# Hybrid SSD and pooling layer with a Strassen feed-forward part: norm and split work, loads and weight buffers moved around the borders of its matmul stages

## The chip, the cores and the metric

The kernel runs on one core of a Trainium2 chip, in one launch. The metric is the device time of that launch in microseconds. The kernel before has a median of 1436.09 us in three runs (1435.75 to 1439.99).

## The reference, cut to what matters

One decoder layer is computed for 1024 prompt positions and 8 sample positions together (1032 columns), with model width 1024, in float32. The changed stages are the output projection's end, the second norm and the feed-forward part.

```python
x = x + jnp.concatenate([y_ssd, y_pool], axis=-1) @ w_out      # 2048 -> 1024
hn = rmsnorm(x, norm2_w)
u = hn @ w_up                                                  # 1024 -> 2 * 2816
u, ffn_new = causal_dwconv(u, ffn_buf, ffn_conv_w, ffn_conv_b) # width 3
gate, val = jnp.split(u, 2, axis=-1)
x = x + (jax.nn.silu(gate) * val) @ w_down                     # 2816 -> 1024
...
y = xf * lax.rsqrt(jnp.mean(xf * xf, axis=-1, keepdims=True) + EPS) * w.astype(jnp.float32)
```

Ahead of these stand the first norm, the input projection, the SSD scan with its gate and norm, and the pooling groups; behind them a last RMSNorm. The outputs also hold the new states.

## The kernel before, in words

Channels lie on the 128 partitions and positions along the free axis. Every float32 operand of a matmul is split in a high part (ACT copies it to the matmul's type: line 210 for moving tiles, 140 for weights) and a low part (DVE subtracts: lines 211 and 141), and each product is three matmuls: high by high, high by low, low by high. Weights go by DMA on SP into `raw` (4 buffers), and their parts into `wop` (4 buffers). The pool `big` has 30 buffers of a tile's width for moving tiles, intermediate tiles and loads; `more` has 6. PSUM gives 8 banks `g` to the feed-forward part.

`w_out` adds its product to x in three parts over eight output tiles n. The first two (SSD heads) take all columns; beside their tiles `down_sums` forms sums of w_down's blocks. The third, `w_out_end`, has the pool groups and runs for one half of the columns (516, in two quarters q of 258) and then for the other. A tile takes 24 matmuls, and then DVE adds each quarter from PSUM to x (line 910). ACT squares the half (917) and sends x to DRAM (`x2d`, 919), and POOL sums the squares for n below 6 (922); the last two go through matmuls with ones. Ln and Exp on ACT give `rn`, and `scale` (943) multiplies x by the norm's weight and by rn on DVE.

The feed-forward part multiplies 2 x 2 blocks with seven products p1 to p7 in place of eight. `moving` makes the sums and splits of the moving blocks; `up_weights` loads weight blocks on SP and adds the second block with an accumulating DMA on POOL (1043); `blocks` has the matmuls (1063). For the first three of 22 pairs j, p1 and p2 of all come first (`up_first`), and then the others. `up_close` makes the convolution (ACT 1137, DVE 1139), SiLU and the product; `spill` makes the differences, and `put` (1160) stores seven blocks per two j in DRAM as `td[0]` to `td[10]`.

`down` reads them back: for each product (p1, p2, p5, p6, p7, p4, p3 in this order) `down_ops` issues eleven loads on POOL (1209) into tiles g and splits them. p1 runs over three slices of the inner dimension (4, 4 and 3 tiles) and within them over four output tiles m; the others go over m first. `down_weights` brings the weights (1227), `piece` the matmuls (1239), and `sink` adds results to x2, which `load_x2` has read back on POOL (1256). The last product interleaves the last norm.

What sets the order: instructions are written down in program order, a scheduler with a simulated time line orders each engine's list, and `behind(ins)` lets an instruction be issued only after `ins` in that order. Each engine then runs its own list strictly in order, and tile pools and operands give the waits between engines.

Of the kernel before, what the change touches and what calls it, by code (L numbers as in the profile page):

```python
# [18 lines left out]
P = 128  # L19
# [56 lines left out]
class Kernel:  # L76
# [131 lines left out]
    def split(self, src, hi, lo, lo_eng=None):  # L208
        nc = self.nc
        nc.scalar.activation(hi, src, AF.Copy)  # L210
        (lo_eng or nc.vector).tensor_tensor(out=lo, in0=src, in1=hi.bitcast(F32), op=ALU.subtract)  # L211

# [636 lines left out]
    def w_out(self, pf):  # L849
# [15 lines left out]
        def part(ops, k0, done=None):  # L865
            for n in range(KT):
                if todo:
                    self.down_sums(len(todo), *todo.pop(0))
# [12 lines left out]
        part(ops, 0)  # L881
# [5 lines left out]
        part(ops, 6)  # L887
# [6 lines left out]
        for t in range(2):  # L894
            self.w_out_end(ops, t)

    def w_out_end(self, ops, t):
# [3 lines left out]
        ssq = self.ph.tile([P, TH], F32, tag=("mh", "sb")[t], name=self.nm("ssq"), bufs=1)  # L901
        pb = [self.bank(b) for b in (("pT", "pT"), ("pM", "pY"))[t]]
        for n in range(KT):
            ws = self.load_tile(d["wout"][n][:, 12 * P : 16 * P], 4)
            x = self.x2[n]
            for q in range(2):
# [3 lines left out]
                nc.vector.tensor_tensor(  # L910
                    out=x[:, lo : lo + TQ], in0=x[:, lo : lo + TQ], in1=ps[:, :TQ], op=ALU.add
                )
            if n == 0:
                act = nc.scalar.activation(ssq, x[:, cols], AF.Square).ins
            else:
                sq = self.ph.tile([P, TH], F32, tag=("sa", "v", "v")[n % 3], name=self.nm("sq"), bufs=(1, 2, 2)[n % 3])
# [19 lines left out]
        if t == 0:  # L936
            for n in range(KT):
                self.scale(n, t)
# [14 lines left out]
    def moving(self, pairs, eng, extra=()):  # L953
# [3 lines left out]
        nc = self.nc  # L957
        ops = {p: [] for p in CHAIN}
# [243 lines left out]
    def down_ops(self, p):  # L1202

        ops = []
        for i in range(0, DK, 2):
# [4 lines left out]
            for j in range(m):  # L1210
                t = self.op_tile()
                self.split(st[:, j], t[:, 0], t[:, 1])
# [31 lines left out]
    def down(self):  # L1244
# [4 lines left out]
        ops = self.down_ops("p1")  # L1249
        x2 = []  # L1250

        def load_x2():
            for n in range(KT):
                t = (self.more if n < 6 else self.big).tile([P, TOK], F32, tag="big", name=self.nm("x2"))
                with self.behind(self.loaded):
                    nc.gpsimd.dma_start(t, self.x2d[n])
                x2.append(t)

        us = [self.big.tile([P, 2, TH], F32, tag="big", name=self.nm("U")) for _ in range(2)]
# [285 lines left out]
```

## Time and profile before

| | |
|---|---|
| median of three runs | 1436.09 us |
| profiled execution, its own time | 1441.22 us |
| its span | 1439.4 us |
| mean granted clock of TensorE | 0.978 |
| PE busy | 1371.8 us (95%) |
| DVE, ACT, POOL busy | 972.9, 700.9, 504.1 us |

PE is the matmul engine, DVE VectorE, ACT ScalarE, POOL GpSimd, SP SyncE. Times of rows are microseconds from the start of the span. In a timeline row the idle time ahead of the instruction and what ended it stand in brackets; "x8" is a run of eight like instructions, and the duration is that of the run. PE matmuls overlap, so a run's duration over its count is nearly the step from one to the next.

### The profile page before, as it was taken

Reading aid. Unit: us, or ns where it says so; the run is one execution under the profiler, and the core shown is the slowest. Engines: PE = TensorE matmul, PEld = TensorE weight load, DVE = VectorE, ACT = ScalarE, POOL = GpSimd, SP = SyncE. Lnnn points to the kernel's source line nnn. Section 1 sums busy time; section 2 is a strip of 40 time slices with the busy share of each in tenths; the row PEclk is TensorE's granted clock in tenths of the full one; section 3 lists DMA queues with packets and bytes.
Section 4 is the critical chain, followed back from the end, with each engine's and each line's share of the span. In section 5 each row is a group of like instructions: output and inputs, shape, how many; then the busy total and the mean of one; then the engine's idle time right before and its main releaser. Section 6 shows DMA issues by size and latency. Waiting matters only on the chain.

```text
span 1439.4 us, 26582 instructions
## 1 busy us (share of the span) xinstructions
PE 1371.8 (95%) x10312; PEld 1321.3 (92%) x10312; DVE 972.9 (68%) x1474; ACT 700.9 (49%) x1408; POOL 504.1 (35%) x569
## 2 busy tenths in 40 slices
PE   8999999797899999999979999999999998999997
PEld 6899878777799999999979999999999998999997
DVE  6475998588863384653678777777777775567743
ACT  6247773366355452311546545554555544544541
POOL 5242576567521104775232222222222213113122
PEclk9999999999899999999989999999999999999999
DMA  6032334334311137776476887878777769457513
GB/s 243 8 99 59 116 122 135 116 121 132 118 36 36 43 91 266 251 224 198 145 206 139 210 207 187 204 187 207 174 184 191 194 219 351 146 182 235 176 47 118
DMA packets 126683, 227.56 MB, mean 158 GB/s; under 512 B 27852, under 2 KB 45084, under 8 KB 126556
## 3 DMA queue, kind: packets, MB, share of 16 engines
q1 hardware_dynamic: 86316, 139.39, 31.2%
q0 software_dynamic: 24208, 61.30, 17.4%
q10 hardware_dynamic: 16032, 25.16, 5.2%
q8 instruction: 81, 1.33, 0.4%
q14 instruction: 46, 0.38, 0.1%
HBM read 169.11 MB, written 45.15 MB: 149 GB/s over the span
## 4 chain that ended last, share of the span: by engine, by line
PE 81%; DVE 9%; DMA 4%; issue 3%; ACT 2%; POOL 1%; SPq 0%; DVEq 0%; ACTq 0%; POOLq 0%
PE g L1063 30%; PE g L1239 16%; PE g L160 10%; PE g L159 10%; PE g L161 10%; DMA mix<-acd 1%; DVE mix L549 1%; DVE mix L504 1%; PE pY L586 1%; DVE xs L482 1%; DVE xs L604 1%; DVE x L295 1%; DMA s<-wup 1%; DVE wop L141 1%; DVE xd L544 1%
## 5 line engine op out<-in xcount | busy, mean ns | idle before, releaser
L1063 PE MATMUL g<-op,wop 128*128 128x258 f32 x3696 | 446.4, 283 | 6.1 <-ACT op L988 5.0
L1063 PEld LDWEIGHTS g<-op,wop 128*128 128x128 f32 x3696 | 445.4, 190 | 6.9 <-ACT op L988 5.2
L1239 PE MATMUL g<-op,wop 128*128 128x258 f32 x1848 | 229.8, 286 | 9.4 <-ACT op L210 5.6
L140 ACT ACTIVATE wop<-raw 128x512 fp32r<-128x512 f32 (+1 forms) x208 | 125.8, 607 | 229.2 <-PE g L161 129.6
L1239 PEld LDWEIGHTS g<-op,wop 128*128 128x128 f32 x1848 | 226.6, 192 | 11.6 <-ACT op L210 6.0
L159 PE MATMUL g<-hh,wop 128*128 128x344 f32 x696 | 227.2, 326 | 4.4 <-ACT u L467 3.8
L161 PE MATMUL g<-hh,wop 128*128 128x344 f32 x696 | 226.5, 325 | 0.0
L160 PE MATMUL g<-hl,wop 128*128 128x344 f32 x696 | 225.7, 324 | 0.0
L141 DVE TENSOR_TENSOR wop<-raw,wop 128x512 fp32r<-128x512 f32 (+1 forms) x186 | 135.9, 736 | 116.2 <-ACT wop L140 111.1
L140 ACT ACTIVATE wop<-s 128x512 fp32r<-128x512 f32 (+1 forms) x136 | 83.4, 620 | 144.3 <-PE g L1063 50.9
L159 PEld LDWEIGHTS g<-hh,wop 128*128 128x128 f32 x696 | 132.8, 191 | 7.4 <-ACT u L467 4.3
L161 PEld LDWEIGHTS g<-hh,wop 128*128 128x128 f32 x696 | 132.7, 191 | 1.3 <-issue 1.1
L160 PEld LDWEIGHTS g<-hl,wop 128*128 128x128 f32 x696 | 133.0, 191 | 0.6 <-issue 0.5
L1043 POOL DMA_DIRECT2D s<-s x44 | 38.3, 870 | 252.3 <-DVE wop L141 106.9
L1139 DVE SCALAR_TENSOR_TENSOR acc<-u,cst,acc 128x1048 f32<-128x1048 f32 x88 | 115.2, 1309 | 12.6 <-ACT acc L1137 11.1
L141 DVE TENSOR_TENSOR wop<-s,wop 128x512 fp32r<-128x512 f32 (+1 forms) x136 | 91.0, 676 | 35.0 <-ACT wop L140 33.2
L1123 DVE TENSOR_TENSOR u<-u,g 128x258 f32<-128x258 f32 (+2 forms) x176 | 58.3, 354 | 74.1 <-PE g L1063 69.9
L1120 ACT ACTIVATE u<-g 128x258 f32<-128x258 f32 (+2 forms) x220 | 69.5, 340 | 71.9 <-PE g L1063 71.7
L160 PE MATMUL g<-yl,wop 128*128 128x344 f32 x288 | 92.6, 323 | 2.3 <-DVE yl L211 2.3
L161 PE MATMUL g<-yh,wop 128*128 128x344 f32 x288 | 92.5, 322 | 0.0
L159 PE MATMUL g<-yh,wop 128*128 128x344 f32 x288 | 91.8, 322 | 0.0
L1209 POOL DMA_DIRECT2D g<-td x77 | 41.9, 548 | 140.6 <-DVE op L211 67.7
(269 smaller groups left out, 2284.6 us busy)
## 6 DMA issues: line engine op xcount, KB each, us to landing
s<-wup SPq DMA_DIRECT2D x88, 256.0 KB, 3.5
g<-td POOLq DMA_DIRECT2D x77, 258.0 KB, 4.6
raw<-wup SPq DMA_DIRECT2D x66, 256.0 KB, 4.1
raw<-win SPq DMA_DIRECT2D x58, 256.0 KB, 2.6
mix<-acd SPq DMA_DIRECT2D x16, 768.0 KB, 5.7
td<-acc ACTq DMA_DIRECT2D x22, 516.0 KB, 6.0
s<-wup POOLq DMA_DIRECT2D x44, 256.0 KB, 5.5
s<-s POOLq DMA_DIRECT2D x44, 256.0 KB, 3.9
```

What stands on the lines that cost most here:

```text
L140: self.nc.scalar.activation(hi, raw[:, :w], AF.Copy)
L141: lo_eng.tensor_tensor(out=lo, in0=raw[:, :w], in1=hi.bitcast(F32), op=ALU.subtract)
L159: nc.tensor.matmul(ps[:, :n], wh, xh[:, sl], start=(first and k == 0), stop=False)
L160: nc.tensor.matmul(ps[:, :n], wh, xl[:, sl], start=False, stop=False)
L161: nc.tensor.matmul(ps[:, :n], wl, xh[:, sl], start=False, stop=(final and k == last))
L1043: nc.gpsimd.dma_start(t, raw[acc] if acc in raw else w[acc][j], accum_op=ALU.add)
L1063: nc.tensor.matmul(out, a, b, start=(p in OPENS and j == 1), stop=(j == 12), skip_group_check=True)
L1120: a = nc.scalar.activation(out, ps[:, s], AF.Copy, scale=-1.0 if p in ("p5", "p4") else 1.0)
L1123: nc.vector.tensor_tensor(out=out, in0=out, in1=ps[:, s], op=op)
L1139: nc.vector.scalar_tensor_tensor(out=acc, in0=u[:, k : k + FW], scalar=self.c("fw", 3 * n + k), in1=acc, op0=ALU.mult, op1=ALU.add)
L1209: self.loaded = self.nc.gpsimd.dma_start(st[:, j], self.td[i + j][ROW[p]]).ins
L1239: self.pe = nc.tensor.matmul(out, a, b, start=(s == 0 and i == 0 and j == 0), stop=(s == len(PIECES) - 1 and i == nk - 1 and j == 2),).ins
```

## The change

- The w_down sums run beside tiles 0 to 5 of w_out's first part and 1 to 6 of its second (before: all eight of the first and four of the second).
- The first half's scales and splits for p1 and p2 run in pairs beside tiles 1 to 7 of the second half, each group issued after the tile's last add; before, the eight scales ran after the first half.
- The squares and their sums use other buffers of the pooling phase.
- The first four moving tiles of p1 of the down projection are loaded and split in `up_close` of the last pair j, before its first convolution step. The rest of p1 follows in `down`, but td[10] only after the first eight loads of p2.
- x2 is read back in half tiles, four halves before p2's last three loads and twelve after; tiles 5 and 7 (before: 6 and 7) are in `big`.
- The first four weight tiles of the last product use the `wop` pool.

```diff
-        def part(ops, k0, done=None):
+        def part(ops, k0, first, done=None):
             for n in range(KT):
-                if todo:
+                if first <= n < first + 6:
                     self.down_sums(len(todo), *todo.pop(0))
...
-        part(ops, 6)
+        part(ops, 6, 1)
...
-        for t in range(2):
-            self.w_out_end(ops, t)
+        self.w_out_end(ops, 0)
+
+        half = KT // 2
+        self.ops = {p: [] for p in CHAIN}
+
+        def beside(n):
+            if n == 0:
+                return
+            for k in {1: (0, 1), 2: (2, 3), 5: (4, 5), 6: (6, 7)}.get(n, ()):
+                self.scale(k, 0)
+            for k in {3: (0, 1), 4: (2, 3), 6: (4, 5), 7: (6, 7)}.get(n, ()):
+                t = self.op_tile()
+                self.split(self.x2[k][:, :TH], t[:, 0], t[:, 1])
+                self.ops["p1" if k < half else "p2"].append((t[:, 0], t[:, 1]))
+
+        self.w_out_end(ops, 1, beside)
...
-        ssq = self.ph.tile([P, TH], F32, tag=("mh", "sb")[t], name=self.nm("ssq"), bufs=1)
+        ssq = self.ph.tile([P, TH], F32, tag=("sb", "ml")[t], name=self.nm("ssq"), bufs=1)
...
-                sq = self.ph.tile([P, TH], F32, tag=("sa", "v", "v")[n % 3], name=self.nm("sq"), bufs=(1, 2, 2)[n % 3])
+                sq = self.ph.tile([P, TH], F32, tag=("mh", "pf", "pf")[n % 3], name=self.nm("sq"), bufs=(1, 2, 2)[n % 3])
...
+            if beside is not None:
+                with self.behind(add):
+                    beside(n)
...
-        if t == 0:
-            for n in range(KT):
-                self.scale(n, t)
...
-        parts("p1", [x[:, a] for x, _ in pairs])
-        parts("p2", [y[:, a] for _, y in pairs])
-        yield ops
...
+        high = None
+        if j == FT - 1:
+            self.begun = self.down_ops("p1", 0, 4)
+            high = self.high
...
-            nc.scalar.activation(acc, u[:, 0:FW], AF.Identity, bias=self.c("fb", n), scale=self.c("fw", 3 * n))
+            with self.behind(high):
+                nc.scalar.activation(acc, u[:, 0:FW], AF.Identity, bias=self.c("fb", n), scale=self.c("fw", 3 * n))
...
-        ops = self.down_ops("p1")
...
+        ops += self.down_ops("p1", len(ops), DK - 1)
+        second = self.down_ops("p2", 0, 8)
+        ops += self.down_ops("p1", DK - 1)
...
-            if p != "p1":
+            if p == "p2":
+                ops = second + self.down_ops(p, len(second))
+                load_x2([(n, t) for n in range(KT) for t in range(2) if (n % 2, t) != (0, 0)])
+            elif p != "p1":
                 ops = self.down_ops(p)
             if p == "p1":
-                load_x2()
+
+                load_x2([(n, 0) for n in range(0, KT, 2)])
...
-                        both[m, s] = self.down_weights(p, m, s, self.big)
+                        both[m, s] = self.down_weights(p, m, s, self.big if m * NS + s >= 4 else None)
```

DVE's list at the start of w_out's second half, before. x_5187 to x_5201 are the eight tiles of x, g the PSUM banks, op the split moving tiles and wop the weights of w_out; the seven rows ahead of these are seven scales like row 604.

```order
604 L943 SCALAR_TENSOR_TENSOR x_5201<-x_5201,cst,rn_6891 128x516
605 L910 TENSOR_TENSOR x_5189<-x_5189,g_6948 128x258
606 L910 TENSOR_TENSOR x_5189<-x_5189,g_6962 128x258
607 L211 TENSOR_TENSOR op_7224<-x_5187,op_7224 128x516
608 L141 TENSOR_TENSOR wop_7093<-raw_7091,wop_7093 128x512
609 L211 TENSOR_TENSOR op_7227<-x_5189,op_7227 128x516
610 L910 TENSOR_TENSOR x_5191<-x_5191,g_6985 128x258
611 L211 TENSOR_TENSOR op_7230<-x_5191,op_7230 128x516
612 L211 TENSOR_TENSOR op_7233<-x_5193,op_7233 128x516
613 L910 TENSOR_TENSOR x_5191<-x_5191,g_6999 128x258
```

The same place after:

```order
597 L925 TENSOR_TENSOR x_5189<-x_5189,g_6940 128x258
598 L925 TENSOR_TENSOR x_5189<-x_5189,g_6954 128x258
599 L958 SCALAR_TENSOR_TENSOR x_5187<-x_5187,cst,rn_6891 128x516
600 L958 SCALAR_TENSOR_TENSOR x_5189<-x_5189,cst,rn_6891 128x516
601 L141 TENSOR_TENSOR wop_7101<-raw_7099,wop_7101 128x512
602 L925 TENSOR_TENSOR x_5191<-x_5191,g_6979 128x258
603 L925 TENSOR_TENSOR x_5191<-x_5191,g_6993 128x258
604 L958 SCALAR_TENSOR_TENSOR x_5191<-x_5191,cst,rn_6891 128x516
605 L958 SCALAR_TENSOR_TENSOR x_5193<-x_5193,cst,rn_6891 128x516
606 L141 TENSOR_TENSOR wop_7140<-raw_7138,wop_7140 128x512
607 L925 TENSOR_TENSOR x_5193<-x_5193,g_7018 128x258
608 L925 TENSOR_TENSOR x_5193<-x_5193,g_7032 128x258
```

The clump of eight scales is gone. Pairs of scales stand behind the adds of tiles 1 and 2 instead, and DVE adds those tiles first.

ACT's list at the border of the up and the down projection, before. acc are the tiles of `up_close` for the last pair, u_12758 and u_12761 its sums out of PSUM, g_13021 the first tile read back and op_13024 its split.

```order
1086 L1120 ACTIVATE u_12761<-g_12785 128x258
1087 L1160 DMA td_13010<-acc_12743 128x516
1088 L188 ACTIVATE acc_12997<-acc_12997 128x1048
1089 L181 ACT_TABLE_LOAD
1090 L1120 ACTIVATE u_12761<-g_12786 128x258
1091 L140 ACTIVATE wop_13188<-raw_13186 128x512
1092 L1137 ACTIVATE acc_13002<-u_12761,cst 128x1048
1093 L210 ACTIVATE op_13024<-g_13021 128x516
1094 L210 ACTIVATE op_13027<-g_13021 128x516
```

The part of the list after in which the first splits for p1 stand (op_12999 to op_13011):

```order
1069 L140 ACTIVATE wop_12907<-s_12777 128x512
1070 L210 ACTIVATE op_12999<-g_12996 128x516
1071 L210 ACTIVATE op_13002<-g_12996 128x516
1072 L140 ACTIVATE wop_12937<-s_12774 128x512
1073 L1131 ACTIVATE u_12761<-g_12847 128x258
1074 L210 ACTIVATE op_13008<-g_13005 128x516
1075 L210 ACTIVATE op_13011<-g_13005 128x516
1076 L1131 ACTIVATE u_12761<-g_12848 128x250
1077 L1131 ACTIVATE u_12761<-g_12848 128x8
1078 L140 ACTIVATE wop_12967<-raw_12780 128x512
1079 L1131 ACTIVATE u_12758<-g_12785 128x258
1080 L1131 ACTIVATE u_12758<-g_12786 128x250
```

The copies L210 stood behind the table load and the last L1137; four of them stand now among the evacuations (L1131, before L1120) of the last up pair.

POOL's list behind p1's loads, before. g are the tiles read back, td_13010 is td[10] and x the tiles of x2.

```order
474 L1209 DMA g_13057<-td_12493 128x516
475 L1209 DMA g_13066<-td_13010 128x516
476 L1256 DMA x_13075<-x2d 128x1032
477 L1256 DMA x_13077<-x2d 128x1032
...
483 L1256 DMA x_13089<-x2d 128x1032
484 L1209 DMA g_13431<-td_7914 128x516
485 L1209 DMA g_13431<-td_8357 128x516
```

And after, where td_13028 is td[10]:

```order
482 L1226 DMA g_13093<-td_11459 128x516
483 L1226 DMA g_13102<-td_13028 128x516
484 L1278 DMA x_13111<-x2d 128x516
485 L1278 DMA x_13113<-x2d 128x516
486 L1278 DMA x_13115<-x2d 128x516
487 L1278 DMA x_13117<-x2d 128x516
488 L1226 DMA g_13459<-td_11976 128x516
489 L1226 DMA g_13459<-td_12493 128x516
```

Before, the load of td[10] and eight loads of x2 stood ahead of p2's first load. Now eight loads of p2 (the last two are shown first) stand ahead of td[10], and x2's halves come behind it.

## Rows read from the trace of the kernel before

**Rows 1.** The page: busy time of each engine, its share of the span, and instructions.

```profile
PE 1371.8 (95%) x10312; PEld 1321.3 (92%) x10312; DVE 972.9 (68%) x1474; ACT 700.9 (49%) x1408; POOL 504.1 (35%) x569
```

**Rows 2.** Waits of PE over the whole span, by what ended them: total us, times, longest.

```profile
PE g L1239 <- ACT op L210: 5.6, 2, 4.1
PE g L1063 <- ACT op L988: 5.0, 1, 5.0
PE g L159 <- DVE x L910: 4.6, 2, 3.3
...
PE g L1239 <- DVE op L211: 1.4, 2, 0.7
```

**Rows 3.** Windows: busy time and number of instructions of each engine, then the granted clock, the DMA engines' busy share and GB/s.

```profile
710.00:720.00 10.00, 7.63 (x62) 7.22 (x60) 10.00 (x16) 6.95 (x19) 4.01 (x2) 1.00 0.28 86
720.00:730.00 10.00, 7.79 (x52) 7.82 (x53) 7.18 (x14) 2.67 (x5) 4.22 (x3) 0.83 0.58 183
750.00:760.00 10.00, 7.63 (x43) 7.63 (x44) 8.97 (x17) 3.47 (x6) 2.04 (x3) 0.66 0.76 150
1150.00:1180.00 30.00, 30.00 (x252) 30.00 (x252) 22.19 (x35) 15.33 (x35) 6.32 (x14) 1.00 0.64 219
1190.00:1200.00 10.00, 7.25 (x39) 6.95 (x40) 9.13 (x13) 3.70 (x6) 6.20 (x13) 0.66 0.91 327
1200.00:1210.00 10.00, 10.00 (x86) 10.00 (x85) 6.29 (x11) 5.76 (x10) 3.16 (x7) 1.00 1.03 405
1390.00:1400.00 10.00, 7.83 (x50) 7.42 (x49) 5.50 (x10) 6.53 (x15) 2.54 (x2) 0.83 0.13 47
```

**Rows 4.** Timeline of PE in the second half of w_out's end: its first matmul, and the two before which PE stood longest.

```profile
705.49 0.47 PE L159 MATMUL g<-ph,wop 128*128 128x258 f32 x1
...
712.87 0.39 PE L159 MATMUL g<-ph,wop 128*128 128x258 f32 x1 [1.26 <-DVE x L910]
...
722.21 0.35 PE L159 MATMUL g<-ph,wop 128*128 128x258 f32 x1 [3.32 <-DVE x L910]
```

**Rows 5.** Timeline of PE at the start of the up projection, and of ACT's copy of accumulated weights there.

```profile
752.37 11.26 PE L1063 MATMUL g<-op,wop 128*128 128x258 f32 x72 [5.03 <-ACT op L988]
...
764.71 1.56 PE L1063 MATMUL g<-op,wop 128*128 128x258 f32 x9 [1.09 <-ACT u L1120]
...
751.16 0.63 ACT L140 ACTIVATE wop<-s 128x512 fp32r<-128x512 f32 x1 [4.88 <-DMA s<-s]
```

**Rows 6.** Timeline of PE from the last up matmuls into the down projection's p1 and p2.

```profile
1186.74 1.23 PE L1063 MATMUL g<-op,wop 128*128 128x258 f32 x9
1192.07 2.09 PE L1239 MATMUL g<-op,wop 128*128 128x258 f32 x8 [4.09 <-ACT op L210]
1194.84 32.37 PE L1239 MATMUL g<-op,wop 128*128 128x258 f32 x256 [0.69 <-DVE op L211]
1228.73 0.74 PE L1239 MATMUL g<-op,wop 128*128 128x258 f32 x4 [1.51 <-ACT op L210]
1230.21 11.55 PE L1239 MATMUL g<-op,wop 128*128 128x258 f32 x92 [0.74 <-DVE op L211]
```

**Rows 7.** Timeline of PE at the start of the last product, and of ACT there.

```profile
1394.82 0.51 PE L1239 MATMUL g<-op,wop 128*128 128x258 f32 x2 [1.95 <-ACT wop L140]
1395.54 5.50 PE L1239 MATMUL g<-op,wop 128*128 128x258 f32 x31 [0.22 <-DVE wop L141]
...
1394.15 3.53 ACT L140 ACTIVATE wop<-s 128x512 fp32r<-128x512 f32 x7
```

**Rows 8.** Timeline of ACT at the end of the up projection, and of POOL's loads of td for p1.

```profile
1188.15 1.28 ACT L181 ACT_TABLE_LOAD   x1
...
1190.25 1.25 ACT L1137 ACTIVATE acc<-u,cst 128x1048 f32<-128x1048 f32 x1
1191.40 1.14 ACT L210 ACTIVATE op<-g 128x516 fp32r<-128x516 f32 x2
...
1169.94 2.21 POOL L1209 DMA_DIRECT2D g<-td  x4 [8.98 <-PE g L1063]
...
1189.49 0.55 POOL L1209 DMA_DIRECT2D g<-td  x1 [11.66 <-DMA td<-acc]
```

**Rows 9.** DMA issues of the page: count, KB each, median us from issue to landing.

```profile
g<-td POOLq DMA_DIRECT2D x77, 258.0 KB, 4.6
```

**Rows 10.** Timeline of DVE in the second half of w_out's end.

```profile
707.06 5.42 DVE L943 SCALAR_TENSOR_TENSOR x<-x,cst,rn 128x516 f32<-128x516 f32 x8 [1.57 <-ACT rn L188]
...
716.76 1.46 DVE L211 TENSOR_TENSOR op<-x,op 128x516 fp32r<-128x516 f32 x1
718.14 1.77 DVE L141 TENSOR_TENSOR wop<-raw,wop 128x512 fp32r<-128x512 f32 x1
...
721.66 0.74 DVE L910 TENSOR_TENSOR x<-x,g 128x258 f32<-128x258 f32 x2
722.32 0.68 DVE L141 TENSOR_TENSOR wop<-raw,wop 128x512 fp32r<-128x512 f32 x1
...
732.62 0.42 DVE L910 TENSOR_TENSOR x<-x,g 128x258 f32<-128x258 f32 x1 [1.01 <-PE g L161]
```

**Rows 11.** Timeline of POOL there: the first two of the five sums of squares, and the last.

```profile
715.28 4.09 POOL L922 TENSOR_TENSOR ssq<-ssq,sq 128x516 f32<-128x516 f32 x2 [18.05 <-ACT sq L917]
...
727.88 1.30 POOL L922 TENSOR_TENSOR ssq<-ssq,sq 128x516 f32<-128x516 f32 x1 [1.68 <-ACT sq L917]
```

More of the change, by code (lines that the diff above doesn't have):

```diff
@@ L209, in split @@
         nc = self.nc
-        nc.scalar.activation(hi, src, AF.Copy)
+        act = nc.scalar.activation(hi, src, AF.Copy).ins
         (lo_eng or nc.vector).tensor_tensor(out=lo, in0=src, in1=hi.bitcast(F32), op=ALU.subtract)
+        return act
     def rsqrt(self, out, sums, scale):
@@ L879, in part @@
                     done(n)
-        part(ops, 0)
+        part(ops, 0, 0)
         ops = []
@@ L893, in w_out, with w_out_end @@
         self.x2d = self.dram.tile([KT, P, TOK], F32, name="x2d")
-        for t in range(2):
-            self.w_out_end(ops, t)
-    def w_out_end(self, ops, t):
+        self.w_out_end(ops, 0)
[11 more added lines that the diff above has]
+        self.w_out_end(ops, 1, beside)
+    def w_out_end(self, ops, t, beside=None):
         nc, d = self.nc, self.d
         cols = slice(t * TH, (t + 1) * TH)
-        ssq = self.ph.tile([P, TH], F32, tag=("mh", "sb")[t], name=self.nm("ssq"), bufs=1)
+        ssq = self.ph.tile([P, TH], F32, tag=("sb", "ml")[t], name=self.nm("ssq"), bufs=1)
         pb = [self.bank(b) for b in (("pT", "pT"), ("pM", "pY"))[t]]
@@ L909, in w_out_end @@
                 self.mm3(ps, ws, ops, lo, TQ)
-                nc.vector.tensor_tensor(
+                add = nc.vector.tensor_tensor(
                     out=x[:, lo : lo + TQ], in0=x[:, lo : lo + TQ], in1=ps[:, :TQ], op=ALU.add
-                )
+                ).ins
             if n == 0:
@@ L953, in moving @@
     def moving(self, pairs, eng, extra=()):
-        nc = self.nc
-        ops = {p: [] for p in CHAIN}
+        nc, ops = self.nc, self.ops
         a, b = slice(0, TH), slice(TH, TOK)
@@ L1200, in down_sums, with down_ops @@
         mix("p3", blk["12"], blk["12"], s2, ALU.subtract)
-    def down_ops(self, p):
+    def down_ops(self, p, first=0, end=DK):
         ops = []
-        for i in range(0, DK, 2):
+        for i in range(first, end, 2):
             m = min(2, DK - i)
@@ L1211, in down_ops @@
                 t = self.op_tile()
-                self.split(st[:, j], t[:, 0], t[:, 1])
+                self.high = self.split(st[:, j], t[:, 0], t[:, 1])
                 ops.append((t[:, 0], t[:, 1]))
@@ L1242, in piece, with down, load_x2 @@
                 ).ins
-    def down(self):
+    def down(self, ops):
         nc, d = self.nc, self.d
         NM, NS = KT // 2, len(PIECES)
-        ops = self.down_ops("p1")
[L1250 to L1254, printed above, removed]
+        ops += self.down_ops("p1", len(ops), DK - 1)
+        second = self.down_ops("p2", 0, 8)
+        ops += self.down_ops("p1", DK - 1)
+        x2 = [None] * KT
+        def load_x2(halves):
+            for n, t in halves:
+                if x2[n] is None:
+                    x2[n] = (self.big if n in (5, 7) else self.more).tile([P, TOK], F32, tag="big", name=self.nm("x2"))
                 with self.behind(self.loaded):
-                    nc.gpsimd.dma_start(t, self.x2d[n])
-                x2.append(t)
+                    self.loaded = nc.gpsimd.dma_start(x2[n][:, half(t)], self.x2d[n][:, half(t)]).ins
+        half = lambda t: slice(t * TH, (t + 1) * TH)
         us = [self.big.tile([P, 2, TH], F32, tag="big", name=self.nm("U")) for _ in range(2)]
-        half = lambda t: slice(t * TH, (t + 1) * TH)
         def sink(p, m, q, ps):
@@ L1417, in phase_ffn @@
                 moving = self.moving([(x2[i], x2[i + half]) for i in range(half)], nc.vector, extra)
+                first = self.up_first(self.ops)
+                next(first)
                 ops = next(moving)
-                first = self.up_first(ops)
-                next(first)
-                next(moving)
                 self.x2 = None
@@ L1428, in phase_ffn @@
                 self.table_set(EXPLN)
-                self.down()
+                self.down(self.begun)
 _INS = {
```

## The prediction

> **What bounds the kernel now.** I read the page first. Its busy line [rows 1] has PE at 1371.8 of 1439.4 us, so PE is idle for 67.6 us, and no other engine is busy for more than 972.9. The kernel is a line of matmuls with holes, and a change is worth what it does to PE's holes and to PE's clock after them. Next, the waits of PE by what ended them [rows 2]. Those in reach of this change are the wait for DVE's adds in w_out (L910, 4.6 us), for the moving tiles of the up projection (ACT L988, 5.0) and for the moving tiles of the down projection (ACT L210, 5.6, DVE L211, 1.4): 16.6 us, and a wait for weight tiles at the last product, told below. In w_out's first two parts, where the w_down sums are moved, the engines' orders are the same in both kernels, so I cost that part at nothing.
>
> Then the windows [rows 3]. A full stretch (1150 to 1180) takes 252 matmuls in 30 us, 0.119 us each; 1200 to 1210 takes 86 in 10, 0.116 each. Behind four of PE's stops, in 720 to 730, 750 to 760, 1190 to 1200 and 1390 to 1400, the granted clock is 0.83, 0.66, 0.66 and 0.83, a mixture of 1.2 and 2.4 GHz. So each of these stops costs more than its idle time. The stops before them lasted 3.32 [rows 4], 5.03 [rows 5], 4.09 [rows 6] and 1.95 us [rows 7]; a stop of 1.26 us [rows 4] was followed by full clock.
>
> **The down border, the largest term.** Before, the last up matmul ends at 1187.97 and the first L1239 starts at 1192.07: 4.09 idle. Eight matmuls then take 2.09 us where 8 x 0.117 = 0.94 would do; 0.69 idle; 256 take 32.37 where 29.95 would do [rows 6]. The loss in p1 is 4.09 + 1.15 + 0.69 + 2.42 = 8.35 us. What PE waits for is ACT's copy of the first moving tile. ACT reaches it at 1191.40 because a table load of 1.28, an evacuation, a weight copy and the 1.25 us activation L1137 stand ahead of it in its order; its data were asked for at 1169.94 [rows 8], where the median load lands in 4.6 us [rows 9]. So it's ACT's order and nothing else. The change moves the first four loads with their copies and subtractions ahead of that group, and interleaves p1's first 24 matmuls with the last up matmuls. PE then has p1's first tiles before it needs them.
>
> Cost of the moved part: four copies at 0.57 [rows 8] and four subtractions at 0.68 (as the lo part in [rows 10]), 2.3 us of ACT and 2.7 of DVE, sooner. In 1150 to 1180 ACT is busy for 15.3 of 30 us and DVE for 22.2 [rows 3], so both have room. But they stand ahead of the last L1137, so the last `up_close`, its spill and td[10] can come up to 2.3 us later. That matters only for the eleventh moving tile, and the change puts this one last and gives p2's eight loads its place in POOL's queue. Before, POOL stood 11.66 us on that td load [rows 8] with x2's loads and all of p2's behind it. After, POOL goes on at once with p2's eight loads, and only then waits.
>
> Next, p2's start: 1.51 + 0.74 = 2.25 us idle, for ACT's and DVE's halves of the split [rows 6]. The loads of these tiles were queued behind x2's eight transfers on POOL. They go ahead of them now, so most of this goes. Against it I set up to 2 us for new short waits, at the third slice of p1 (which needs td[10]) or where U is evacuated in a clump. Sum here: 8.35 + 2.25 = 10.6 at most, and I take 9.5; the lower bound is 4.1, if td[10] comes late enough for a new stop like the old one in p1's third slice, with the half clock behind it: 10.6 - 4.09 - 2.42.
>
> **The last product.** Before, PE stands for 1.95 and 0.22 us at 1394.82, and 31 matmuls take 5.50 us where 3.6 would do [rows 7]: 4.1 us. ACT makes the weight copies in a run of seven from 1394.15, 3.53 us [rows 7]; by its order they wait for large tiles that the product before gives back. Four of twelve weight tiles now come from the pool of weight buffers, which are free once p4 has passed them, so the first tile's weights and one of the next are ready. The fifth still comes behind the release: about 1.1 us of wait (two copies at 0.5) stays. I take 2.5; bounds 1 (the same wait, one tile on) and 4.1.
>
> **The norm border.** Before, DVE runs eight scales in one clump of 5.42 us, and then eight splits and the weights' lo parts between the adds [rows 10]. PE stands 1.26 us at 712.87 and 3.32 us at 722.21 [rows 4], both for an add that came late, and goes on at half clock for some 3 us (about 1.5 lost). All that could be gained by spreading is 1.26 + 3.32 + 1.5 = 6.1 us. But DVE's work isn't less. For the eight tiles of the second half it is 16 adds at 0.37, and eight lo parts, eight scales and eight splits at 0.68 [rows 10]: 5.9 + 16.3 = 22.2 us, against PE's 8 x 2.86 = 22.8 (24 matmuls at 0.119). Where tiles 1, 2 and 5 carry a pair of scales DVE needs 0.74 + 0.68 + 1.36 = 2.8, and for tile 6 with both pairs 4.1. And a DVE instruction beside a POOL sum of squares takes 1.46 or 1.77 us instead of 0.68 [rows 10], so 0.78 to 1.09 more, with five such sums in the half [rows 11]: up to 5 x 0.93 = 4.7, 26.9 in all. In before the loop runs from 705.5 [rows 4] to the end of the last add, 732.62 + 0.42 [rows 10]: 27.5 us. Going through the new order tile by tile I get 23.6 us to the last add where DVE never blocks PE, 25.7 with half of the prolongations and 28.0 with all. Since DVE's instructions now lie closer to POOL's sums (two scales or two splits at every tile from 1 on), I take a value between the last two, 27. That is 0.5 gained; bounds -0.6 and +3.8. The other squares' buffers free the loads of the first up weights from a wait on PE and ACT, but the 5.03 us at 752.37 hang on accumulated weights whose transfer ends at 751.16 [rows 5], a chain that starts when raw buffers come free behind the loop's last lo part. It stays, and moves with the loop. The 1.09 us at 764.71 [rows 5] go half, as p3's weight copy no longer stands ahead of the evacuation. Sum: 1 us; bounds -1.5 and +5.
>
> The Trainium skill, "SBUF — State Buffer", section "SBUF: two separate sides", says that VectorE with two SBUF inputs and a GpSimd instruction that reads SBUF lock each other out of a shared port pair for the whole of an instruction. The two prolonged rows and the POOL pair of 4.09 us (1.30 for one alone) agree with a lock. By this rule each of the five sums could hold DVE for its whole 1.30, 6.5 in all, 28.7 us of DVE work, and the border would gain nothing, where the rows give up to 4.7.
>
> **The sum.** 1 + 9.5 + 2.5 = 13.0 us off the profiled execution: span 1439.4, run 1441.2, so 1428.2 for a run like it. The median of the runs is 1436.09, 5.1 below the profiled run, and the stages that change have no part in that as far as one profile tells; so 1436.1 - 13 = 1423.
>
> **Rivals.**
> - *The norm border opens too.* If POOL's sums seldom meet DVE's two-input instructions, the loop comes near PE's 23.6 us: 3.8 more, and with the whole of the 1.09 and of the last product's 4.1 the gain is 17 to 21: 1415 to 1419. For it: before has DVE busy for only 7.18 us of 720 to 730 [rows 3]. Against it: the load that falls on tile 6, and five sums.
> - *Part of the down border comes back.* ACT's order at the last pair is longer by four copies; if td[10] or the clump of U's evacuations stops PE for 2 to 4 us, the border gives 4 to 6 instead of 9.5, and with nothing at the norm the gain is 4.3 to 8.5: 1428 to 1432. For it: DMA's share is 1.03 in 1200 to 1210, in the stretch in which td[10] is stored and read back [rows 3]. Against it: two thirds of p1, over 20 us of matmuls, stand ahead of the tile's first use.
> - *Nothing in the end.* The stop is only moved: the last up pair's evacuation stands on ACT behind copies that wait for their loads, PE stops there for some 4 us with half clock (8 in all), and 2 to 3 us are left, within 0.3%: 1432 to 1440.
> - *Slower.* One mechanism: in ACT's order the four moved copies stand ahead of evacuations of the last up pair; a load of td that lands after the copy's turn stops ACT, then PE, which has no free PSUM bank. With the median landing of 4.6 us [rows 9] that can't be, as these parts of td were stored over 10 us before; from a landing about 12 us later than that it costs more than the 13 us gained: 1441 and up.
>
> **How the numbers follow.** The forecast (a gain of 8.5 to 17; own range 1419 to 1428) has 0.56, the norm border open 0.12, part given back 0.18, nothing 0.09, slower 0.05. What a measurement can tell from no change is 0.3%, 4.3 us. Faster: 0.56 + 0.12 + 0.18 = 0.86; same 0.09; slower 0.05. The range takes in the forecast, the two rivals beside it and, for the bounds of the terms, a microsecond more at both ends: 1414 to 1433.
>
> **What would show it.** Right: no L1256 matmul waits over 1 us for ACT L210 at the border, the clock there is 1.00, and the window after the last up matmul holds some 85 matmuls per 10 us; POOL's long wait for td stands after p2's loads. In the w_out end, PE's waits for the add are many and short, or one, and together near 5 us; the 5 us for accumulated weights stay. In the last product one wait near 1.1 us, at full clock. Wrong: a stop with half clock anywhere in p1, or a last add at the norm border under 25 us or over 28 us after the half's first matmul.

## The result, and the profile after

The changed kernel takes 1421.78 us (median of four runs, 1417.24 to 1425.72); the kernel before, with a fourth run beside the three told of above, 1438.04 (1435.75 to 1440.89). The ratio is 0.9878, with a 95% interval of 0.985 to 0.9907: 16.3 us less. The forecast was 1423, 13.0 us less. On another chip, five more runs of the changed kernel gave 1423.24 against 1438.52, a ratio of 0.9891 (0.9871 to 0.991), or 15.3 us less. The profiled execution has a span of 1421.1 us, and 1422.84 as its own time.

The waits of PE after, by what ended them (total us, times, longest); they answer to [rows 2]:

```profile
PE pM L940 <- ACT sq L932: 4.3, 2, 2.7
...
PE g L1074 <- ACT op L999: 1.7, 1, 1.7
PE g L1256 <- ACT op L210: 1.7, 1, 1.7
PE g L160 <- DVE yl L211: 1.6, 1, 1.6
PE g L1074 <- DVE op L1004: 1.6, 2, 0.8
PE g L1074 <- DVE u L1134: 1.4, 1, 1.4
...
PE g L1256 <- ACT wop L140: 0.5, 1, 0.5
PE g L159 <- DVE x L925: 0.5, 1, 0.5
```

The wait of the down projection's matmuls (L1256, before L1239) for ACT's split fell from 5.6 to 1.7 us, that for its weights to 0.5. The wait for w_out's adds fell from 4.6 to 0.5, but 4.3 us for the squares of tiles 6 and 7 stand in its place. The wait for ACT's accumulated-weights chain at the start of the up projection (op L999, before L988) fell from 5.0 to 1.7, but waits there for DVE (op L1004 and u L1134, 3.0 us in all) are new; before, one of 1.09 us for ACT stood in their place [rows 5]. PE's stops at the norm border, from the last two tiles' squares on:

```profile
724.97 0.70 PE L940 MATMUL pM<-sq,ones 128*128 128x258 f32 x2 [1.59 <-ACT sq L932]
...
728.78 1.23 PE L940 MATMUL pM<-sq,ones 128*128 128x258 f32 x2 [2.67 <-ACT sq L932]
...
746.38 3.39 PE L1074 MATMUL g<-op,wop 128*128 128x258 f32 x26 [1.72 <-ACT op L999]
750.51 0.98 PE L1074 MATMUL g<-op,wop 128*128 128x258 f32 x6 [0.74 <-DVE op L1004]
...
752.33 5.04 PE L1074 MATMUL g<-op,wop 128*128 128x258 f32 x40 [0.84 <-DVE op L1004]
...
758.78 3.40 PE L1074 MATMUL g<-op,wop 128*128 128x258 f32 x26 [1.42 <-DVE u L1134]
```

The timeline of PE at the down border, which answers to [rows 6]:

```profile
1178.72 1.60 PE L1256 MATMUL g<-op,wop 128*128 128x258 f32 x12
1180.15 1.60 PE L1074 MATMUL g<-op,wop 128*128 128x258 f32 x12
1181.59 0.76 PE L1256 MATMUL g<-op,wop 128*128 128x258 f32 x5
1182.19 1.60 PE L1074 MATMUL g<-op,wop 128*128 128x258 f32 x12
1183.62 36.57 PE L1256 MATMUL g<-op,wop 128*128 128x258 f32 x303
1221.86 13.35 PE L1256 MATMUL g<-op,wop 128*128 128x258 f32 x109 [1.68 <-ACT op L210]
```

No row of p1 has a bracket: its 264 matmuls run without a stop, 17 of them between the last up matmuls and the others behind, at 0.12 us a step. One stop of 1.68 us is left in p2.

The last product, as [rows 7]:

```profile
1379.46 0.51 PE L1256 MATMUL g<-op,wop 128*128 128x258 f32 x2 [0.53 <-ACT wop L140]
1380.18 2.54 PE L1256 MATMUL g<-op,wop 128*128 128x258 f32 x19 [0.22 <-DVE wop L141]
```

The stop of 1.95 us is one of 0.53, and it stands one weight tile later: 21 matmuls of the second output tile follow it, 33 before. Windows, with columns as in [rows 3]:

```profile
720.00:730.00 10.00, 5.46 (x31) 4.65 (x32) 9.82 (x17) 6.25 (x17) 1.64 (x1) 0.84 0.49 152
730.00:740.00 10.00, 10.00 (x66) 9.44 (x65) 5.93 (x10) 6.96 (x17) 2.71 (x3) 0.81 0.97 269
...
1190.00:1200.00 10.00, 10.00 (x85) 10.00 (x85) 8.22 (x15) 4.04 (x8) 4.86 (x9) 1.00 0.93 294
...
1380.00:1390.00 10.00, 9.82 (x75) 9.59 (x76) 7.42 (x14) 6.61 (x16) 1.73 (x4) 1.00 0.16 51
```

The down border and the last product are at full clock; of the changed stages, the norm border alone still has half clock in it (0.84 and 0.81).

Three marks cut the span into stages. The first is the matmul at 705.49 before and 702.16 after. [rows 4] and the prediction call it the first of w_out's second half, but it begins the half's second tile (tile 1): 168 matmuls, seven tiles, lie between it and the first up matmul, and tile 0's run ahead of it. These seven tiles are called the loop below. The second mark is the start of the 169th up matmul. The third is the end of the 33rd matmul of the last product, from where its second output tile could begin; in the changed kernel it lies 12 matmuls, 1.44 us, ahead of the stop shown above. "Again" is a second profile of the same program. The last column is what the prediction took off.

| stage, us | before | after | again | measured gain | forecast |
|---|---|---|---|---|---|
| start to the first mark | 705.49 | 702.16 | 704.29 | 3.3, 1.2 | 0 |
| to the 169th up matmul (norm border) | 59.22 | 56.62 | 56.60 | 2.6 | 1 |
| to the last product's second tile (down border in it) | 628.16 | 618.71 | 617.21 | 9.5, 11.0 | 9.5 |
| to PE's last matmul (last product) | 37.55 | 34.58 | 34.57 | 3.0 | 2.5 |
| rest | 9.0 | 9.0 | 9.0 | 0 | 0 |

Of the 2.6 us at the norm border, 0.1 lie ahead of the first up matmul and 2.5 behind it. There PE stands for 4.7 us in place of 6.1, which is 1.4; the other 1.1 is a faster pace of its matmuls: the granted clock in 750 to 760 is 1.00, where before had 0.66 [rows 3].

### The profile page after: what moved, and what is told of

It is laid out like the page before. It is cut to its first block, busy times and chain, and to the rows that moved or that the text cites. A ratio compares the mean times of both kernels' runs of the same rounds, so it can differ in the third digit from the quotient of the medians.

```text
span 1421.1 us, 26585 instructions
## 1 busy us (share of the span) xinstructions
PE 1364.8 (96%) x10312; PEld 1313.3 (92%) x10312; DVE 968.7 (68%) x1474; ACT 701.1 (49%) x1408; POOL 504.5 (36%) x577
## 4 chain that ended last, share of the span: by engine, by line
PE 79%; DVE 10%; DMA 4%; issue 3%; POOL 2%; ACT 1%; SPq 0%; DVEq 0%; ACTq 0%; POOLq 0%
PE g L1074 30%; PE g L1256 15%; PE g L160 10%; PE g L161 10%; PE g L159 10%; DMA mix<-acd 1%; DVE wop L141 1%; DVE xs L483 1%; DVE mix L550 1%; PE pY L587 1%; DMA st<-st_ssm 1%; DVE x L296 1%; DVE xs L605 1%; DVE mix L505 1%; POOL st L639 1%
## 5 line engine op out<-in xcount | busy, mean ns | idle before, releaser
L1256 PE MATMUL g<-op,wop 128*128 128x258 f32 x1848 | 225.2, 283 | 2.4 <-ACT op L210 1.7
L1256 PEld LDWEIGHTS g<-op,wop 128*128 128x128 f32 x1848 | 222.7, 189 | 3.5 <-ACT op L210 1.9
L141 DVE TENSOR_TENSOR wop<-raw,wop 128x512 fp32r<-128x512 f32 (+1 forms) x186 | 141.3, 765 | 110.5 <-ACT wop L140 108.3
L1156 DVE SCALAR_TENSOR_TENSOR acc<-u,cst,acc 128x1048 f32<-128x1048 f32 x88 | 115.2, 1309 | 12.2 <-ACT acc L1154 10.6
L1134 DVE TENSOR_TENSOR u<-u,g 128x258 f32<-128x258 f32 (+2 forms) x176 | 58.0, 354 | 72.9 <-PE g L1074 66.1
L1131 ACT ACTIVATE u<-g 128x258 f32<-128x258 f32 (+2 forms) x220 | 69.6, 340 | 70.7 <-PE g L1074 70.6
```

Source lines behind the costliest of these rows:

```text
L141: lo_eng.tensor_tensor(out=lo, in0=raw[:, :w], in1=hi.bitcast(F32), op=ALU.subtract)
L1131: a = nc.scalar.activation(out, ps[:, s], AF.Copy, scale=-1.0 if p in ("p5", "p4") else 1.0)
L1134: nc.vector.tensor_tensor(out=out, in0=out, in1=ps[:, s], op=op)
L1156: nc.vector.scalar_tensor_tensor(out=acc, in0=u[:, k : k + FW], scalar=self.c("fw", 3 * n + k), in1=acc, op0=ALU.mult, op1=ALU.add)
L1256: self.pe = nc.tensor.matmul(out, a, b, start=(s == 0 and i == 0 and j == 0), stop=(s == len(PIECES) - 1 and i == nk - 1 and j == 2),).ins
```

## The experiments

Six of these kernels ran once each, for their profile: the sums back (1425.06 us), p2's early loads undone (1428.09), the last product's weight tiles (1424.79), spreading (1430.13), the buffers (1422.62) and p4's loads alone (1423.64). For these the stages are compared, not the run times.

**Is the first stage's difference the w_down sums' doing?** All engines' orders up to there are the same, but the profile after is 3.3 us ahead. One run puts the sums back, and one repeats the changed kernel.

```diff
-                if first <= n < first + 6:
+                if todo:
```

> The changed kernel with the w_down sums beside w_out's tiles where they were before (eight and four). The engines' orders are those of the changed kernel. Theory (the 3.3 us by which the changed kernel's profile is ahead at the first matmul of w_out's second half are chance): all stages behind that point last as in the changed kernel within 0.5 us; ahead of it PE's wait for yl L211 may be anywhere between 1.6 and 2.4 us and the point between 702 and 706. Rival (the moved sums shorten that wait): the wait is 2.3 us and the clock behind it 0.83 again, the point at 705.5.

> The changed kernel itself once more. Its profile, as a second one of the same program, shows how far single stages differ by chance: the first matmul of w_out's second half between 700 and 708 us, PE's wait for op L999 between 1.5 and 4 us, all stages of the down projection within 2 us of the first profile. Run time 1419 to 1426.

With the sums put back, the first mark comes at 704.97, and the wait for yl L211 is 3.04 us, where 1.6 to 2.4 were expected; all stages behind are within 0.5 us of the changed kernel's but two: the 169th up matmul comes at 57.78 for 56.62, and the down stage takes 616.74 for 618.71. The 0.5 us were too narrow. The repeat has 704.29, a wait of 1.95 and a clock of 0.83 behind it. Over the twelve profiles of the changed kernel and its variants, which have the same orders up to there, the mark lies between 700.83 and 707.81, and the wait is at most 3.04; before's 705.49 and 2.32 are inside. So differences of this size come by chance; the moved sums show no effect, as forecast. The expectation of the repeat missed at one place: the wait for op L999 was 1.24, not 1.5 to 4.

**The early copies.** All of p1's tiles back in `down`, the rest unchanged:

```diff
-            self.begun = self.down_ops("p1", 0, 4)
-            high = self.high
+            self.begun = []
```

> The changed kernel without the four early moving tiles of p1: all eleven are loaded and split in the down projection's own part, p2's eight loads still ahead of td[10]. Theory (the stop at the down border was ACT's order, and the early copies removed it): PE waits again for ACT op L210 at the first L1256 for 3.5 to 4.5 us, the clock behind it falls to 0.6 to 0.7 in a 10 us window, and the run is 6 to 9 us slower than the changed kernel. Rival (the stop went because POOL and DMA were freed of x2's loads): the wait stays under 1 us.

Median 1430.43 us (1428.01 to 1433.28), ratio to before 0.9935 (0.9911 to 0.9959): 8.7 us slower than the changed kernel's 1421.78, and 7.2 slower than its second median. Against the kernel before in the same rounds (1440.56) the gain is 10.1 us, where the changed kernel had 16.3 and 15.3, so 5 to 6 us are lost. PE and ACT at the border, and the window behind it:

```profile
1187.88 1.78 PE L1255 MATMUL g<-op,wop 128*128 128x258 f32 x8 [4.09 <-ACT op L210]
1190.66 69.54 PE L1255 MATMUL g<-op,wop 128*128 128x258 f32 x561 [0.99 <-DVE op L211]
```

```profile
1186.06 1.25 ACT L1153 ACTIVATE acc<-u,cst 128x1048 f32<-128x1048 f32 x1
1187.21 1.14 ACT L210 ACTIVATE op<-g 128x516 fp32r<-128x516 f32 x2
```

```profile
1190.00:1200.00 10.00, 9.34 (x61) 9.35 (x62) 8.06 (x13) 3.30 (x6) 3.78 (x7) 0.74 0.64 187
```

The stop of 4.09 is back to the hundredth, ended by the same copy behind the same L1153, with half clock after it: 0.74 in the window, where 0.6 to 0.7 was expected. The down stage takes 624.7 us, 6.8 more than the mean of the two changed profiles (618.0); in the ten profiles that have this border as changed it takes 616.7 to 618.7. The theory holds.

**p2's loads ahead of td[10] and x2.** Here td[10] and all halves of x2 come first on POOL:

```diff
-        ops += self.down_ops("p1", len(ops), DK - 1)
-        second = self.down_ops("p2", 0, 8)
-        ops += self.down_ops("p1", DK - 1)
+        ops += self.down_ops("p1", len(ops))
...
-                load_x2([(n, 0) for n in range(0, KT, 2)])
+                load_x2([(n, t) for n in range(KT) for t in range(2)])
```

> The changed kernel with td[10] and all of x2 loaded ahead of p2's tiles on POOL, as before; x2 still in halves. Theory (p2's early loads are worth the 2.25 us of waits that p2's start had): PE waits for ACT or DVE at p2's start for 2 to 5 us in all, where the changed kernel has 1.7. Rival (they are worth little, since the changed kernel has 1.7 us there still): the wait stays at 1 to 2 us and the span from the last up matmul to p2's hundredth is within 1 us.

PE at p2's start:

```profile
1218.57 0.74 PE L1256 MATMUL g<-op,wop 128*128 128x258 f32 x4 [1.51 <-ACT op L210]
1220.05 11.29 PE L1256 MATMUL g<-op,wop 128*128 128x258 f32 x92 [0.74 <-DVE op L211]
```

These are before's two waits, 1.51 and 0.74, unchanged. The down stage takes 620.1 us, 2.1 more than the mean of the two changed profiles and 1.4 more than the longest of those ten. The order of POOL's queue is what removed them. What stays at this place in the changed kernel is 1.68 us in one profile, 0.20 in the next and none with the sums put back. In the profile that has 1.68 the cause is another: ACT stands for a weight transfer there, and the split of p2's tile is queued behind that copy.

```profile
1220.66 0.63 ACT L140 ACTIVATE wop<-raw 128x512 fp32r<-128x512 f32 x1 [4.13 <-DMA raw<-wdn]
```

**The last product's weight tiles.** All of them back in the large pool:

```diff
-                        both[m, s] = self.down_weights(p, m, s, self.big if m * NS + s >= 4 else None)
+                        both[m, s] = self.down_weights(p, m, s, self.big)
```

> The changed kernel with all of the last product's weight tiles in the large pool, as before. Theory (the four tiles in the weight pool took away most of the stop and with it the half clock): PE waits 1.9 to 2.2 us for the second output tile's weights, the granted clock behind it is below 0.9 in a 10 us window, and from the wait's end to the last matmul the stretch is as in the kernel before; the last product is 2.5 to 3.5 us longer than the changed kernel's. Rival (the early loads of the down projection's start moved that stop too): the wait stays at 0.5 to 0.8 us.

PE and two windows:

```profile
1378.73 5.88 PE L1256 MATMUL g<-op,wop 128*128 128x258 f32 x33 [1.94 <-ACT wop L140]
```

```profile
1370.00:1380.00 10.00, 8.06 (x61) 7.63 (x61) 2.57 (x6) 3.82 (x8) 2.57 (x2) 0.93 0.00 1
1380.00:1390.00 10.00, 10.00 (x73) 9.80 (x71) 6.48 (x13) 6.61 (x16) 0.99 (x2) 0.89 0.17 48
```

The stop is 1.94 us again, with half clock behind it, and from the second tile to the last matmul it takes 37.15 us for 34.58: 2.6 us are these four tiles'.

**The norm border: spreading.** The eight scales back in a clump, the splits where before had them, other buffers kept:

```diff
-        self.w_out_end(ops, 1, beside)
+        for k in range(KT):
+            self.scale(k, 0)
+        self.w_out_end(ops, 1)
...
+        parts("p1", [x[:, a] for x, _ in pairs])
+        parts("p2", [y[:, a] for _, y in pairs])
+        yield ops
```

> The changed kernel with the first half's eight scales in one clump behind the first half, and the splits where before had them; buffers and all else as changed. Theory (spreading only moves DVE's work, since DVE and POOL's sums bound the loop): from the first matmul of the second half to the first up matmul 29.5 to 30.5 us, as in both kernels, with one or two waits for the add of 1 to 3.5 us in place of the waits for squares; what is gained behind it stays. Rival (the spreading is what gained at this border): the stretch up to the 169th up matmul is 2 us or more longer than the 56.6 us of the changed kernel.

From the first mark to the first up matmul it takes 30.02 us (29.87 changed, 30.00 before), with waits of 1.28 and 3.36 us for an add, as in before (1.26 and 3.32). The 169th up matmul comes at 58.73, 2.1 us later than in the changed kernel; so the rival's bound is met. But with the sums put back the same mark came at 57.78 in the changed kernel's orders, so only 1 to 2 us can be put down to spreading. It gains nothing up to the first up matmul, as the theory said, but this much behind it, which the theory did not say: the wait for the accumulated weights is 4.77 us here. The last lo part of w_out's weights starts 27.8 us after the first mark with the clump, and 27.0 without, and the chain of transfers starts behind it, the seven s loads at 28.9 and 28.1.

**The norm border: the buffers.** Only the tags of the squares and their sums as before; the orders are those of the changed kernel.

```diff
-        ssq = self.ph.tile([P, TH], F32, tag=("sb", "ml")[t], name=self.nm("ssq"), bufs=1)
+        ssq = self.ph.tile([P, TH], F32, tag=("mh", "sb")[t], name=self.nm("ssq"), bufs=1)
...
-                sq = self.ph.tile([P, TH], F32, tag=("mh", "pf", "pf")[n % 3], name=self.nm("sq"), bufs=(1, 2, 2)[n % 3])
+                sq = self.ph.tile([P, TH], F32, tag=("sa", "v", "v")[n % 3], name=self.nm("sq"), bufs=(1, 2, 2)[n % 3])
```

> The changed kernel with the squares and their sums in the buffers of before; the engines' orders are the same, only waits differ. Theory (the first accumulating transfers on POOL no longer wait for PE and ACT, and that is why PE's wait for the accumulated weights fell from 5.03 to 1.72 us): the second L1054 transfer waits again for ACT u, 2 us or more, and PE's wait for op L999 is 3.5 to 5 us. Rival (the wait fell because the loop's last lo part came earlier and PE ran at half clock): it stays between 1.5 and 2.2 us.

POOL's second accumulating transfer waits for PE, 1.49 us (2 or more, and for ACT, were expected), PE's wait is 3.65, and the 169th up matmul comes at 58.28. The row on POOL:

```profile
734.90 0.90 POOL L1054 DMA_DIRECT2D s<-wup  x1 [1.49 <-PE g L1074]
```

PE's wait lies in the theory's 3.5 to 5, but its mechanism isn't shown. This transfer is issued 33.85 us after the first mark, and in the six profiles that have the new buffers in the changed kernel's orders it is issued at 33.3 to 34.3: the wait for PE doesn't make it later. And with the sums put back, a kernel with the new buffers, PE's wait was 3.24 and the mark 57.78. At most 0.5 to 1.7 us could be this edit's, and no run shows that it gains anything.

**What bounds the loop.** The second half's squares are summed on PE instead of by POOL:

```diff
-                if n < 6:
+                if t == 0 and n < 6:
...
-                            pb[q][:, :TQ], self.ones, sq[:, q * TQ : (q + 1) * TQ], start=(n == 6), stop=False
+                            pb[q][:, :TQ], self.ones, sq[:, q * TQ : (q + 1) * TQ], start=(n == (1 if t else 6)), stop=False
```

> The changed kernel with the second half's squares summed by matmuls with ones on PE (as tiles 6 and 7 are) in place of POOL's five sums; DVE's order is the same. Theory (each POOL sum holds the DVE lo part beside it for some 1.1 us): the five lo parts of 1.80 us take 0.68, DVE's part of the loop is 5.6 us shorter, PE has ten matmuls of 0.25 more, the waits for squares of 1.59 and 2.67 us shrink to 1 us or less each, and the first up matmul comes 27 to 28 us after the loop's first (29.9 in the changed kernel); run time 2 to 4 us less. Rival (the lo parts are long for another reason, as their raw weights landing late): they stay at 1.8 us and the stretch grows to 30 to 32 us.

First the changed kernel, DVE and POOL at the first sum; then this kernel's DVE at the same place, and its PE:

```profile
707.10 1.80 DVE L141 TENSOR_TENSOR wop<-raw,wop 128x512 fp32r<-128x512 f32 x1
```

```profile
706.66 1.69 POOL L937 TENSOR_TENSOR ssq<-ssq,sq 128x516 f32<-128x516 f32 x1 [12.77 <-ACT sq L932]
```

```profile
705.77 0.69 DVE L141 TENSOR_TENSOR wop<-raw,wop 128x512 fp32r<-128x512 f32 x1
...
725.46 0.42 DVE L925 TENSOR_TENSOR x<-x,g 128x258 f32<-128x258 f32 x1
726.59 0.42 DVE L925 TENSOR_TENSOR x<-x,g 128x258 f32<-128x258 f32 x1 [0.72 <-PE g L161]
```

```profile
727.80 0.70 PE L940 MATMUL pM<-sq,ones 128*128 128x258 f32 x2 [1.24 <-ACT sq L932]
...
729.45 6.79 PE L1074 MATMUL g<-op,wop 128*128 128x258 f32 x54
735.73 5.57 PE L1074 MATMUL g<-op,wop 128*128 128x258 f32 x45
746.10 6.11 PE L1074 MATMUL g<-op,wop 128*128 128x258 f32 x34 [4.80 <-ACT op L999]
```

All lo parts take 0.68 or 0.69 without POOL's sums, so the rival is out; DVE now waits for PE, and the wait for squares is one of 1.24. The trace has 20 more matmuls with ones, at 0.22 us a step, and the last add ends at 26.2 us, no earlier than the changed kernel's 25.8: here PE bounds the loop. The first up matmul comes at 28.62 us, a little later than the 27 to 28 expected. But the run is not faster, 1421.50 us (1419.69 to 1424.46), and its ratio to the kernel before is 0.9882, the changed kernel's 0.9878: the wait for the accumulated weights grew to 4.80, and the 169th up matmul comes at 56.74. What the loop gained, the next wait took.

**That wait.** p4's plain load, in the first three pairs, goes behind the loads of weights to be summed; alone, and with the squares on PE:

```diff
+        last = None
...
-            nc.sync.dma_start(t, w[first][j])
+            with self.behind(None if acc is not None or j >= NEARLY else last):
+                ins = nc.sync.dma_start(t, w[first][j]).ins
+            last = ins if acc is not None else last
```

> The changed kernel, but for the first three pairs of the up projection the plain load of p4's weights is issued on SP behind the loads of the weights to be summed. Theory (PE's wait for op L999 at the start of the up projection is for a chain of transfers that starts when SP gets past two plain loads which wait for free raw buffers): the seven s<-wup loads start 25 to 26 us after the first matmul of w_out's second half in place of 28.1, ACT's copy of the accumulated weights at 40 to 42 in place of 43.0 and 44.3 in the two profiles of the changed kernel's orders, and PE's wait for it falls under 1 us. Rival (the chain is limited by DMA, whose share is over 1.0 there): the copy stays at 43 to 45 and the wait at 1.7 to 3.3 us.

> Both edits: squares of the second half summed on PE, and p4's plain loads behind the loads to be summed. Theory: the first up matmul 28.6 us after the loop's first as with the squares on PE alone, and the wait for op L999 falls from the 4.8 us there to 1 to 2.5; the run is 2 to 5 us faster than the changed kernel. Rival (DMA limits the chain): the wait stays over 4 us and the run is within 2 us of the changed kernel.

> Squares of the second half summed on PE, and p4's plain loads behind the loads to be summed, on the same chip and in the same rounds as the changed kernel. Theory (the border between w_out and the up projection is 1.5 to 2.6 us shorter, the rest the same): median 1 to 4 us below the changed kernel's. Rival (given back by DVE, which is busy all the time behind it): within 1 us of it.

SP, ACT and PE with the loads alone:

```profile
729.13 1.94 SPq L1054 DMA_DIRECT2D s<-wup  x4
```

```profile
746.26 0.63 ACT L140 ACTIVATE wop<-s 128x512 fp32r<-128x512 f32 x1 [1.98 <-PE g L1077]
```

```profile
747.47 0.50 PE L1077 MATMUL g<-op,wop 128*128 128x258 f32 x2 [1.24 <-ACT op L999]
```

The loads start 25.3 us after the first mark, as expected. ACT's copy waits for a weight buffer from PE and not for a transfer, but it comes at 42.5, and PE's wait is 1.24, not under 1. The second profile of the changed kernel has the same without this edit, a copy at 42.8 that waits 1.98 us for PE and then a stop of 1.24, so alone it shows no effect. The 169th up matmul is at 56.62, as in the changed kernel: behind the chain stands DVE, which has the up projection's moving tiles to make and is busy for all of 740 to 760. With both edits PE's wait for the accumulated weights is 1.45 and 1.46 us in two profiles, where the squares on PE alone had 4.80, and the mark comes at 55.16 in each, 1.5 us earlier. The first set of runs gave 1421.49 us (1418.17 to 1424.02), not to be told from the changed kernel; 2 to 5 us had been expected. In the second, on one chip and in the same rounds, five runs gave 1421.77 (1417.51 to 1422.84) against 1423.24 (1423.02 to 1423.96): 1.5 us, and no run of one lies among those of the other. It is the fastest version of that set, by 0.1%.

## Why the prediction was right, and where it was not

- **The down border, forecast 9.5.** Right in mechanism and size: 9.5 and 11.0 in two profiles, 6.8 lost without the early copies and 2.1 without p2's early loads. The stop was ACT's order; it was removed and nothing took its place in p1. That one profile gained more than my upper bound of 10.6 is within what this long stage differs by from profile to profile (616.7 to 618.7). The "up to 2 us for new short waits" were 0 to 1.7, and the place I named for them was wrong: neither td[10] nor U, but p2's start.
- **The last product, forecast 2.5.** 2.6 by undoing it, 3.0 between the profiles. The wait that stays was 0.53 us, where I had 1.1.
- **The norm border, forecast 1, measured 2.6.** This is the term that was mis-sized. Up to the first up matmul 0.13 us were gained, where I had 0.5, but not as I had it. My sums of 22.2 us for DVE and 22.8 for PE count eight tiles, and the 27.5 us that I set them against hold seven, so they were too long by a tile. By my prices, what DVE does from the first mark to the last add (14 adds, eight scales, six splits and six lo parts) is 18.8 us, and a sum on POOL cost it 1.12 (1.80 less 0.68), where I had 0.93 from before's rows. The last add ended at 25.8 us, better than the 27 I took. PE lost this again: it stopped 1.59 and 2.67 us for the last two tiles' squares, which I had at nothing, and ran its last eight matmuls with ones at half clock. The waits for an add, near 5 us in my signs, were one of 0.47. So the 0.13 beside my 0.5 is luck. My step "It stays, and moves with the loop", on the 5.03 us for the accumulated weights, failed. The last lo part came 0.8 us earlier, which starts the chain earlier; I had seen this and not priced it. The wait fell to between 1.2 and 3.2 us in the profiles that have the changed kernel's orders and buffers. Why it differs so much among them stays open. My 0.5 for the evacuation's 1.09 failed too: there PE waits for DVE now, 1.42 us, behind two waits of 0.74 and 0.84.
- **The rule on the shared port.** The Trainium skill, "SBUF — State Buffer", section "SBUF: two separate sides", holds here: the lo part that began at 707.10 ended at 708.90, 0.55 us after POOL's sum, as if it had stood until POOL was done. With no sums on POOL the prolongation is gone. The rule's own sum, no gain in the loop, was nearer to the 0.13 measured than mine, but by luck: by its 28.7 us of DVE work the last add would have come later than I had it, and it came earlier.
- **The base.** The profile before is 3.3 us behind the profile after in a stage that the change doesn't touch. I was right to give this stage nothing, but the median that I set out from, 1436.09, is 2 us under that of four runs. So 1423 came closer to 1421.78 than its terms did, and that is luck: they were 2.3 to 3.3 us short of the gain. The three changed stages' gains add up to 15.1 and 16.6 us in the two profiles, and the runs gained 16.3 and 15.3.
- **The rivals.** Neither a stop by ACT's longer order in the last up pair nor a late td[10] came: PE's rows from 1178.72 to the end of p1 have no wait. The rival of a part given back began at a gain of 4.3 us, where its own terms (4 to 6, and 2.5) begin at 6.5.

## What to carry to other kernels

Where an engine's list is run in order, a matmul can stop for work whose data arrived long ago: look for what stands ahead of it in the list of the engine that it waits for, and move the work before that. A wait that a change shortens is worth only the distance to the next one. Here the seven profiles in which PE waited 1.2 to 2.8 us for the accumulated weights all took 26.5 to 26.8 us from the first up matmul to the 169th, with DVE's work as the next limit; with waits of 3.2 us and more it took 27.9 to 29.2. Before reading a difference of one profile stage by stage, take a second profile of the same program.

## What the runs showed of the hardware

- Stages ahead of any change differed by up to 7.0 us between profiles of equal instruction orders (700.83 to 707.81), though five runs of one kernel on one chip lay within 1 us (1423.02 to 1423.96).
- Stops of one length left TensorE's granted clock at either level. After a stop of 1.95 us for yl it fell to 0.83 in the next 10 us in the second profile of the changed kernel, and stayed at 1.00 in the kernels with p4's loads alone and with the last product's weight tiles back in the large pool. With both edits at the norm border, a stop of 1.45 us was followed by 0.95 and 0.88 in 740 to 760 in one profile, and one of 1.46 by 1.00 in the other. After 1.64 us (yl) and 1.68 (p2) it stayed at 1.00. So a stop's length alone doesn't tell.
- A prolonged DVE instruction beside a POOL one isn't slowed evenly: it ends a nearly fixed time after POOL's, 0.55 us for each of the five sums in the changed kernel's profile.
